# A one-core decoder layer: a v tile's transfer ahead of its slot's others, latent fetches in pairs, and a half swap behind q's parts

## The chip, the cores and the metric

The kernel runs on one core of one Trainium2 chip. A core has a matrix engine (TensorE, PE in the profile, with PEld for its weight loads), VectorE (DVE), ScalarE (ACT), GpSimd (POOL), and SyncE (SP), which here does nothing but issue transfers. The engines run their own instruction streams in order and wait for each other through semaphores; transfers are carried out by 16 DMA engines. The metric is the time of one execution on the device in microseconds, as the median of several runs.

## The reference

One layer of a decoder over 512 tokens of width 2048, in float32. What matters here:

```python
h = rmsnorm(x, attn_norm_g) * (1.0 + scale) + shift          # scale, shift, gate from silu(c) @ w_ada + b_ada
q_lat, kv_lat, k_rope, z_mla, u, v, z_sgu, g_mla, g_sgu = split_cols(h @ w_in, IN_SPLITS)
q  = rmsnorm(q_lat, q_norm_g) @ w_uq        # 16 heads of 128 plain + 64 rotary columns
kv = rmsnorm(kv_lat, kv_norm_g) @ w_ukv     # 16 heads of 128 (k) + 128 (v)
y_mla = causal_attention(q, k, v) * silu(z_mla)
vn = rmsnorm(v, sgu_norm_g)                 # 16 groups of 128 columns, 4 chunks of 128 tokens
mixed = einsum('gts,bnsgd->bntgd', tril(w_spatial), vn) + b_spatial
y_sgu = u * mixed * silu(z_sgu)
x = x + gate * ((sigmoid(g_mla) * y_mla + sigmoid(g_sgu) * y_sgu) @ w_out)
return rmsnorm(x, final_norm_g)
```

The rotary part swaps the halves of each head's 64 columns: `[t1*cos - t2*sin, t2*cos + t1*sin]`.

## The kernel before

Every product is made in float32 precision out of three matmuls on a high and a low part of each operand. For each weight tile ACT casts the high part (`L629` in the mixing loop, `L118` in the streamed stages) and DVE subtracts it to make the low part (`L136`, `L119`); PE then runs high x high, low x high, high x low. So PE needs, for each weight tile, first ACT and then DVE to be done.

The work goes in stages:

- The first two products over all of `x`: the latents of q and k/v, and the columns that a block of the next stage would not hold. They leave for DRAM.
- **The mixing loop** (`L1352` to `L1388`): 11 blocks of weight columns (v, u, the gates) in a seven-product scheme of the Strassen kind, with 28 steps each. A step is 12 matmuls of 128x512 on one weight tile (`L1384` to `L1386`). The weights come through buffers `X0`, `X1`, `X5` (blocks that pass), `X4` and `wraw0` to `wraw2` (blocks that are kept and added to). Their parts go to `w0`, `w1` and one more pair of `X` buffers in rotation.
- Between the steps lie side jobs: the 16 groups of the gating unit, bias sums, rotary tables, and the normalisation of the latents. A side job is put at a step and a phase with `on(step, phase, f)`. In each step `run` goes through FIRST, HIGH, EVAC, GATE, SPLIT, BACK before the step's matmuls are recorded, and through MISC and LOAD after them. What is recorded first stands first in its engine's queue. `place` looks for a step with room on DVE, by a table of costs. Nothing else orders the work: the engines run what they were given in that order.
- **Attention** over 16 heads, with weights through a stream of three raw buffers (`Stream`), then the output product and the last norm.

A group g of the gating unit has these parts: `gain_load` and `v_load` fetch a gain row and a 128x512 tile of v from DRAM (`v_d`), four steps later `sgu_scale` (ACT, `L928`) multiplies v by its norm, DVE multiplies the group's spatial weights by a triangle (`sgu_weights`, `wsr`) which ACT and DVE split, DVE multiplies by the gain, and `sgu_split` makes `sinT` and `vl`, v's high and low parts. `sgu_mix` is one product of three matmuls on PE, in phase MISC. All groups use one buffer for v, `lat12`: the next `v_load` has to wait until DVE has made `vl` of the group before. It is put at the step of that group's mix, in phase LOAD, in which weight transfers of the mixing loop are issued as well.

The normalised latents (ten tiles of 128x512, `latn_d`) are fetched back by `lat_fetch` from step `s_att` on, which is step -11 counted from the loop's end, and split by `lat_split` (ACT `L1313`, DVE `L139`) in the last seven steps; 8 and 9 follow behind the loop. The last weight block of the loop is issued at step -9. At the loop's end SP also issues the rotary tables, the shared rotary key (`kr_d`) and the first weights of attention.

The first head pair begins with `rproj(0)` (rotary queries), `qproj(0)`, `kproj(0)` and `vproj(0)`. `qproj` takes its weights, calls `meanwhile`, records its 18 matmuls, calls `then`, and records q's high and low parts:

```python
    def swapped(m2, src):
        for b in range(4):
            s_, d_ = slice(32 * b, 32 * b + 32), slice(32 * (b ^ 1), 32 * (b ^ 1) + 32)
            ACT.copy(m2[d_], src[s_])
```

SP's transfers also share eight completion semaphores in rotation, so that a transfer waits for the landing of the one eight before it.

Of the kernel before, what the change touches and what calls it, by code (L numbers as in the profile page):

```python
# [128 lines left out]
def trunk_layer(ctx, tc, xT, xn, c, vecs, pos, wada, w1, w2, wv, wv3, wv4, wh, wh15, wq, wqr, wk, wvv, wo, wsT, bsp, gfin, out,  # L129
# [17 lines left out]
    def mm3(ps, ah, al, bh, bl, start, stop):  # L147
        PE.matmul(ps, ah, bh, start=start, stop=False)  # L148
        PE.matmul(ps, ah, bl, start=False, stop=False)  # L149
        PE.matmul(ps, al, bh, start=False, stop=stop)  # L150

    def hilo(hi, lo, src):
        ACT.copy(hi, src)
        tt(lo, src, hi.bitcast(F32), ALU.subtract)
# [28 lines left out]
    ws = Stream(nc, [(wp, f"wraw{i}") for i in range(3)], [(wp, f"w{i}") for i in range(2)])  # L183
# [83 lines left out]
    gq, gr, gk, gvv = {}, {}, {}, {}  # L267
# [45 lines left out]
    def get(i, ahead=1, run=1):  # L313
        r = ws.get(i, ahead)
        fs, pend[:] = pend[:run], pend[run:]
        for f in fs:
            f()
        return r
# [11 lines left out]
    def bank():  # L330
        n_bank[0] += 1
        return bank_at(ring[(n_bank[0] - 1) % len(ring)])
# [368 lines left out]
    FIRST, HIGH, EVAC, GATE, SPLIT, BACK, MISC, LOAD = range(8)  # L701

    def on(s, phase, f, *a):
        assert s >= done[0], (s, done)
        events.setdefault(s, {}).setdefault(phase, []).append(lambda: f(*a))
# [7 lines left out]
    def place(s, us, f, *a):  # L713

        def full(s):
            own, (a, b) = busy.get(s, 0.0) + us, (busy.get(s + d, 0.0) for d in (-1, 1))
            near = [sum(busy.get(s + d + k, 0.0) for k in range(5)) for d in range(-4, 1)]
            return own > 3.3 or own + max(a, b) > 5.75 or s < at_block[T0] + 22 and max(near) + us > 13.4

        while full(s):  # L720
            s += 1
        spend(s, us)
        on(s, BACK, f, *a)
        return s
# [141 lines left out]
    last_gates = []  # L866
    for b in range(1, len(BLOCKS)):
# [21 lines left out]
        if ta == "z":  # L889
            for half in range(2):  # L890
                s_ = max(ready[ta, ca, half], ready[tb_, cb, half]) + 1
# [68 lines left out]
    for c in range(4):  # L960
        for half in range(2):
            s_ = ready["u", c, half]
            for ty in sorted("st", key=lambda t: ready[t, c, half]):
                s_ = place(max(s_, ready[ty, c, half]) + 1, 1.22, t_gate, c, ty, half)
                gated[ty, c, half] = s_
            gated[c, half] = s_
    s_ = at_block[T0] + 6
    on(s_, LOAD, sgu_load, 0)
    out_at = {-2: s_, -1: s_}
    for g in range(H):  # L970
        c, q = divmod(g, 4)
        on(s_, LOAD, gain_load, g)
        on(s_, LOAD, v_load, g)
        a = s_ + 4
        on(a, BACK, sgu_scale)
        a = place(a, 0.29, sgu_weights)
        a = place(a, 0.29, sgu_weights_split)
        if g + 1 < H:
            on(a + 1, LOAD, sgu_load, g + 1)
        a = place(max(a, s_ + 5), 0.69, sgu_gain)  # L980
        a = place(a + 1, 0.69, sgu_split)
        s_ = max(a + 1, out_at[g - 2], max(ready["u", c, half] for half in range(2)) - 2)
        on(s_, MISC, sgu_mix, g)
        for half in range(2):
            out_at[g] = place(max(s_ + 1, ready["u", c, half] + 1), 0.46, sgu_out, g, half)
            last_out[g, half] = out_at[g]
        if q == 3:
            for half in range(2):
                stored[c, half] = max(last_out[k, half] for k in range(4 * c, g + 1)) + 1
                stored[c, half] = max(stored[c, half], gated[c, half] + 1)  # L990
                on(stored[c, half], LOAD, t_store, c, half)
# [143 lines left out]
    def to_bias(s, q):  # L1135

        on(s, MISC, shift_turn, 4 * q)
        return place(s + 1, 0.6, shift_sum, 4 * q)

    used, biased = [rope_end + 3] * 3, []  # L1140
    s_ = used[0]
    for i, (q, ks, _) in enumerate(shares):
        on(used[-3], LOAD, share_load, i)
        s_ = place(max(used[-3] + 4, s_ + 1), 0.75 if len(ks) == 1 else 1.4, share, i)
        used.append(s_)
        if ks[-1] == KC - 1:
            s_ = to_bias(s_ + 1, q)
# [66 lines left out]
    s_ = s_rx + 4  # L1214
    for group in (((10, "lat8"), (11, "lat9")), ((12, "lat10"), ("plain", "sinT"))):
        for i, t in group:
            on(free_at[t], LOAD, lat_load, i, t, z_d if i == "plain" else None)
        for i, _ in group:
            if i == "plain":
                s_ = place(s_ + 1, 0.69, plain_gate)  # L1220
            else:
                s_ = place(max(s_, s_bias) + 1, 0.69, lat_scale, i)
                on(s_ + 1, BACK, last_sigmoid, i)
                s_ = place(s_ + 2, 0.69, last_gate, i)
        i = group[0][0]
# [3 lines left out]
    for lo_, hi_, dim in ((0, 6, 768), (6, 10, 512)):  # L1229
# [6 lines left out]
        for i in range(lo_, hi_):  # L1236
            s_ = place(max(loaded[i] + 4, s_ + 1), 0.69, lat_scale, i)
# [3 lines left out]
        s_ = added  # L1241
        on(s_ + 1, MISC, lat_sums, dim)
        s_ = place(s_ + 2, 1.3, lat_recip)
        s_ += 1
        on(s_, MISC, lat_rstd)
        for i in range(lo_, hi_):
            s_ = place(s_ + 1, 0.75, lat_norm, i)
# [33 lines left out]
# [5 lines that stand above are left out]
# [7 lines left out]
    s_ = s_lat + 1  # L1293
    on(s_, LOAD, key_load)
    s_ += 5
    for i in range(3):
        s_ = place(s_ + 1, 0.69, key_rotary, i)
# [35 lines left out]
    s_att = max(V7.index((2, 3)) + 1 - n_v, s_lat + 1)  # L1333
    on(s_att, LOAD, to_attention)
    for i in range(10):
        on(s_att + i // 3, LOAD, lat_fetch, i)
        if i < 8:
            on((-7, -7, -5, -5, -3, -3, -2, -2)[i], BACK, lat_split, i)

# [67 lines left out]
    def at(name, dt, shape=(P, S)):  # L1407
        p, tag = place[name]
        if p is latp.p:
            v = slot(tag, dt)  # L1410
            return v if len(shape) == 2 else v.rearrange("p (n w) -> p n w", n=shape[1])
        return nt(p, list(shape), dt, tag)
# [67 lines left out]
    def qproj(h, meanwhile=None, then=None):  # L1480
        wH, wL = get(gq[h])
        if meanwhile:
            meanwhile()
        ps = bank()
        for k in range(6):
            sl = slice(k * P, (k + 1) * P)
            mm3(ps, wH[:, sl], wL[:, sl], lh[k], ll[k], k == 0, k == 5)
        if then:
            then()
        qh, ql = at("qh", F32R), at("ql", F32R)  # L1490
        hilo(qh, ql, ps)
        qt[h] = (qh, ql)

    def rproj(p):
        wH, wL = get(gr[p])
        ps = bank_at(0)
        for k in range(6):
            sl = slice(k * P, (k + 1) * P)
            mm3(ps, wH[:, sl], wL[:, sl], lh[k], ll[k], k == 0, k == 5)
        return ps  # L1500
# [12 lines left out]
    def kproj(h):  # L1513
        wH, wL = get(gk[h])
        ps = bank()
        for k in range(4):
            sl = slice(k * P, (k + 1) * P)
            mm3(ps, wH[:, sl], wL[:, sl], lh[6 + k], ll[6 + k], k == 0, k == 3)
        return ps
# [127 lines left out]
    fetch(0)  # L1647
    rps = rproj(0)
    m2 = at("m2", F32)
    qproj(0, lambda: (swapped(m2, rps), [f() for f in last_gates]), lambda: ws.split_to(gvv[0]))  # L1650
    ps = kproj(0)
    kfinish(0, ps)
    rfinish(0, rps, m2)
# [12 lines left out]
    for h in range(H):  # L1666
# [8 lines left out]
        if more:  # L1675
            qproj(h + 1, lambda: merge(1 if h == H - 2 else None))
            if not odd and 2 * pair < H:
                rps = rproj(pair)
# [33 lines left out]
        if not odd and 2 * pair < H:  # L1712
            m2 = at("m2", F32)
# [69 lines left out]
    def residual(n, part, sl, ps, last=False):  # L1783
        y = yt[:, n, sl]
        w = sl.stop - sl.start
        t = nt(tp, [P, S], F32, "sig", bufs=3)[:, :w]
        tt(t, ps, grow[:, sl], ALU.mult)
        tt(y, t, y, ALU.add)
        junk = nt(tp, [P, S], F32, "sig", bufs=3)[:, :w]
        ACT.activation(junk, y, AF.Square, accum_out=ssy[:, n, part:part + 1])  # L1790
        if not last:
            tt(y, y, gfb[:, sl], ALU.mult)

    for cg in range(3):
# [6 lines left out]
        for n in range(NB):  # L1801
            f = lambda n=n, cg=cg, ps=pso[n]: residual(n, cg, slice(cg * 512, (cg + 1) * 512), ps)
# [107 lines left out]
```

## Time and profile before

| | |
|---|---|
| median of 3 runs | 1571.46 us (1569.64 to 1572.58) |
| profiled execution, its own time | 1570.91 us |
| its span, first to last instruction | 1569.2 us |
| mean granted TensorE clock | 0.998 |
| moved from and to HBM | 291.11 MB read, 23.68 MB written |

In the profile's rows the first number is the start in microseconds from the span's start, the second the duration, then engine, line of the kernel, operation, `out<-in`, shape and count. In square brackets stands how long the engine was idle before the row and what ended that. Rows of SPq are transfers being issued: their duration is that of the issue, not of the transfer. The chain of work that ended last follows PE through most of the span.

### The profile page before, as it was taken

What the parts mean: (1) busy time and instruction counts of PE and PEld (TensorE: products, weight loads), DVE (VectorE), ACT (ScalarE), POOL (GpSimd) and SP (SyncE); (2) the same over time, 40 slices, a digit from 0 to 9 for tenths busy, and PEclk for the clock granted to TensorE, in tenths of its full rate; (3) what the DMA queues carried; (4) which work ended last, traced back from release to release, by engine and by line L of the source; (5) the groups of instructions that cost most, each with busy time, mean ns of one, the idle gap of its engine ahead of it and who ended that gap; (6) DMA issues with size and microseconds to landing.
All of it is one profiled execution on the core that took longest, in us unless ns stands there. A gap on an engine that the chain in (4) does not pass through costs nothing.

```text
span 1569.2 us, 20577 instructions
## 1 busy us (share of the span) xinstructions
PE 1554.3 (99%) x7392; PEld 1297.0 (83%) x7392; DVE 1218.4 (78%) x1667; ACT 803.1 (51%) x1238; POOL 69.8 (4%) x67
## 2 busy tenths in 40 slices
PE   9999999999999999999999999999999999999998
PEld 8888778888888888888788888887888888888887
DVE  8989777678887879788879797878777777865763
ACT  4445555546545555445455565657655565532332
POOL 0000000201010101020100010100000000000000
PEclk9999999999999999999999999999999999999999
DMA  9989565949795968686867685966443433348722
GB/s 378 374 278 346 162 192 159 246 131 260 214 241 162 244 203 227 196 230 188 226 178 204 204 251 161 260 166 207 152 118 116 130 118 118 93 133 332 264 89 107
DMA packets 237224, 316.16 MB, mean 201 GB/s; under 512 B 16201, under 2 KB 184193, under 8 KB 231489
## 3 DMA queue, kind: packets, MB, share of 16 engines
q1 hardware_dynamic: 214210, 291.78, 56.7%
q0 software_dynamic: 22912, 23.07, 9.5%
q8 instruction: 58, 0.95, 0.3%
q14 instruction: 44, 0.36, 0.1%
HBM read 291.11 MB, written 23.68 MB: 201 GB/s over the span
## 4 chain that ended last, share of the span: by engine, by line
PE 60%; DVE 2%; DMA 2%; ACT 1%; issue 1%; SPq 0%; DVEq 0%; ACTq 0%
PE ps L1386 10%; PE ps L1384 10%; PE ps L1385 10%; PE ps L149 9%; PE ps L150 9%; PE ps L148 9%; PE ps L1600 1%; PE ps L1626 1%; DMA X<-in_wh 1%; PE ps L1560 1%; PE ps L1561 1%; DMA lat<-v_d 0%; DVE d L136 0%; DMA rx<-kr_d 0%; DVE w1l L136 0%
## 5 line engine op out<-in xcount | busy, mean ns | idle before, releaser
L136 DVE TENSOR_TENSOR X<-X,X 128x1024 fp32r<-128x1024 f32 (+2 forms) x111 | 130.5, 1182 | 31.1 <-ACT X L629 29.5
L629 ACT CAST X<-X 128x1024 fp32r<-128x1024 f32 x70 | 73.7, 1052 | 98.1 <-PE ps L1385 60.9
L629 ACT CAST w0h<-X 128x1024 fp32r<-128x1024 f32 x70 | 73.7, 1052 | 98.0 <-PE ps L1385 49.2
L629 ACT CAST w1h<-X 128x1024 fp32r<-128x1024 f32 x69 | 72.6, 1052 | 75.1 <-PE ps L1385 40.8
L136 DVE TENSOR_TENSOR w0l<-X,w0h 128x1024 fp32r<-128x1024 f32 x70 | 85.5, 1222 | 29.4 <-ACT w0h L629 29.2
L136 DVE TENSOR_TENSOR w1l<-X,w1h 128x1024 fp32r<-128x1024 f32 x69 | 84.3, 1221 | 24.7 <-ACT w1h L629 24.6
L136 DVE TENSOR_TENSOR X<-wraw,X 128x1024 f32<-128x1024 f32 (+1 forms) x65 | 79.4, 1221 | 20.8 <-ACT X L629 18.4
L119 DVE TENSOR_TENSOR w0l<-wraw,w0h 128x1024 fp32r<-128x1024 f32 (+4 forms) x61 | 64.2, 1053 | 40.3 <-ACT w0h L118 38.3
L118 ACT CAST w1h<-wraw 128x1024 fp32r<-128x1024 f32 (+4 forms) x60 | 50.5, 841 | 84.2 <-PE ps L150 21.9
L1386 PE MATMUL ps<-w1l,hh 128*128 128x512 f32 x236 | 92.0, 390 | 1.5 <-DVE w1l L136 1.4
L118 ACT CAST w0h<-wraw 128x1024 fp32r<-128x1024 f32 (+4 forms) x61 | 56.0, 918 | 72.4 <-PE ps L150 21.1
L1386 PE MATMUL ps<-X,hh 128*128 128x512 f32 x232 | 90.6, 391 | 1.5 <-DVE X L136 1.5
L1384 PE MATMUL ps<-w1h,hh 128*128 128x512 f32 x236 | 92.0, 390 | 0.0
L1385 PE MATMUL ps<-w1h,hl 128*128 128x512 f32 x236 | 91.9, 389 | 0.0
L1385 PE MATMUL ps<-w0h,hl 128*128 128x512 f32 x236 | 91.8, 389 | 0.0
L1384 PE MATMUL ps<-w0h,hh 128*128 128x512 f32 x236 | 91.8, 389 | 0.0
L1386 PE MATMUL ps<-w0l,hh 128*128 128x512 f32 x236 | 91.8, 389 | 0.0
L1384 PE MATMUL ps<-X,hh 128*128 128x512 f32 x232 | 90.4, 390 | 0.0
L1385 PE MATMUL ps<-X,hl 128*128 128x512 f32 x232 | 90.3, 389 | 0.0
L139 DVE SCALAR_TENSOR_TENSOR wada<-wada,cact 128x2048 f32<-128x2048 f32 x39 | 88.9, 2282 | 0.6 <-DMA wada<-in_wada 0.6
L119 DVE TENSOR_TENSOR w1l<-wraw,w1h 128x1024 fp32r<-128x1024 f32 (+4 forms) x60 | 57.4, 957 | 34.3 <-ACT w1h L118 33.4
L148 PE MATMUL ps<-hh,w1h 128*128 128x512 f32 x204 | 81.3, 399 | 0.0
(410 smaller groups left out, 4419.7 us busy)
## 6 DMA issues: line engine op xcount, KB each, us to landing
X<-in_wh SPq DMA_DIRECT2D x131, 512.0 KB, 5.0
wada<-in_wada SPq DMA_DIRECT2D x39, 1024.0 KB, 7.6
wraw<-in_wo SPq DMA_DIRECT2D x32, 512.0 KB, 4.1
wraw<-in_wh SPq DMA_DIRECT2D x21, 512.0 KB, 5.5
wraw<-in_wh POOLq DMA_DIRECT2D x21, 512.0 KB, 7.2
X<-in_wv SPq DMA_DIRECT2D x17, 512.0 KB, 3.7
X<-in_wh SPq DMA_DIRECT2D x22, 384.0 KB, 5.2
wraw<-in_w SPq DMA_DIRECT2D x16, 512.0 KB, 9.7
```

What stands on the lines that cost most here:

```text
L118: self.nc.scalar.copy(hi[:, :n], raw[:, :n])
L119: self.nc.vector.tensor_tensor(out=lo[:, :n], in0=raw[:, :n], in1=hi[:, :n].bitcast(F32), op=ALU.subtract)
L136: DVE.tensor_tensor(out=out, in0=in0, in1=in1, op=op)
L139: DVE.scalar_tensor_tensor(out=out, in0=in0, scalar=scalar, in1=in1, op0=op0, op1=op1, **kw)
L148: PE.matmul(ps, ah, bh, start=start, stop=False)
L149: PE.matmul(ps, ah, bl, start=False, stop=False)
L150: PE.matmul(ps, al, bh, start=False, stop=stop)
L629: ACT.copy(hi, t)
L1384: PE.matmul(ps[t].rearrange("p (h w) -> p h w", h=4), xh[:, tk], wH[:, k], start=st, stop=False, skip_group_check=True)
L1385: PE.matmul(ps[t].rearrange("p (h w) -> p h w", h=4), xl[:, tk], wH[:, k], start=False, stop=False, skip_group_check=True)
L1386: PE.matmul(ps[t].rearrange("p (h w) -> p h w", h=4), xh[:, tk], wL[:, k], start=False, stop=sp, skip_group_check=True)
L1560: PE.matmul(ps, q2[:, q], krh[:, :n], start=False, stop=False)
```

## The change

Three places are edited.

```diff
     for g in range(H):
         c, q = divmod(g, 4)
+        on(s_, MISC, v_load, g)
         on(s_, LOAD, gain_load, g)
-        on(s_, LOAD, v_load, g)
...
     for i in range(10):
-        on(s_att + i // 3, LOAD, lat_fetch, i)
+        on(s_att + (0, 0, 2, 2, 4, 4, 5, 5, 6, 6)[i], LOAD, lat_fetch, i)
...
-    qproj(0, lambda: (swapped(m2, rps), [f() for f in last_gates]), lambda: ws.split_to(gvv[0]))
+    qproj(0, lambda: [f() for f in last_gates], lambda: ws.split_to(gvv[0]))
+    swapped(m2, rps)
```

First, `v_load` goes from phase LOAD to phase MISC of the same step, so that it is issued ahead of every other transfer of that step. In SP's queue it changes places with the gain row in every group, with weight transfers in nine (1, 3, 4, 7, 8, 9, 11, 12 and 15), with the spatial weights in group 0, and with a store of `t_d` in groups 5 and 13. In SP's queue group 12 (the transfer from `v_d`) stood behind two weight tiles in four transfers and the gain row:

```order
L1012 DMA half0_932_6268<-in_wh 128x512
L594 DMA wraw1_936_6291<-in_wh 128x3x256
L599 DMA wraw1_936_6291<-in_wh15 128x2x128
L594 DMA X5_937_6294<-in_wh 128x3x256
L599 DMA X5_937_6294<-in_wh15 128x2x128
L910 DMA gsr_938_6297<-gain_row_107 128x128
L914 DMA lat12_939_6299<-v_d_111 128x4x128
L594 DMA X0_942_6319<-in_wh 128x3x256
```

and stands now right behind the transfer of the bias sums (`half0`):

```order
L1012 DMA half0_932_6268<-in_wh 128x512
L914 DMA lat12_936_6291<-v_d_111 128x4x128
L594 DMA wraw1_937_6293<-in_wh 128x3x256
L599 DMA wraw1_937_6293<-in_wh15 128x2x128
L594 DMA X5_938_6296<-in_wh 128x3x256
L599 DMA X5_938_6296<-in_wh15 128x2x128
L910 DMA gsr_939_6299<-gain_row_107 128x128
L594 DMA X0_942_6319<-in_wh 128x3x256
```

The v transfer has moved ahead by five transfers; the order of the others is unchanged.

Second, the ten latents are fetched two at a time over seven steps instead of three at a time over four. In SP's queue (`b6` to `b15` are the latents' tiles, `X1` the mixing loop's last weight block, `wraw0` takes the rope-query weights, `wraw1` q's) stood before

```order
L1306 DMA b6_1318_8613<-latn_d0_127 128x512
L1306 DMA b7_1319_8615<-latn_d1_128 128x512
L1306 DMA b8_1320_8617<-latn_d2_129 128x512
L1306 DMA b9_1323_8637<-latn_d3_130 128x512
L1306 DMA b10_1324_8639<-latn_d4_131 128x512
L1306 DMA b11_1325_8641<-latn_d5_132 128x512
L594 DMA X1_1328_8661<-in_wh 128x4x256
L1306 DMA b12_1329_8663<-latn_d6_133 128x512
L1306 DMA b13_1330_8665<-latn_d7_134 128x512
L1306 DMA b14_1331_8667<-latn_d8_135 128x512
L1306 DMA b15_1336_8689<-latn_d9_136 128x512
L99 DMA wraw0_48_8717<-in_wqr 128x768
```

and now

```order
L1306 DMA b6_1318_8613<-latn_d0_127 128x512
L1306 DMA b7_1319_8615<-latn_d1_128 128x512
L594 DMA X1_1324_8653<-in_wh 128x4x256
L1306 DMA b8_1325_8655<-latn_d2_129 128x512
L1306 DMA b9_1326_8657<-latn_d3_130 128x512
L1306 DMA b10_1337_8705<-latn_d4_131 128x512
L1306 DMA b11_1338_8707<-latn_d5_132 128x512
L99 DMA wraw0_48_8709<-in_wqr 128x768
L1306 DMA b12_1341_8727<-latn_d6_133 128x512
L1306 DMA b13_1342_8729<-latn_d7_134 128x512
L1306 DMA b14_1349_8761<-latn_d8_135 128x512
L1306 DMA b15_1350_8763<-latn_d9_136 128x512
```

The weight block stands behind two latents instead of six, and the rope-query weights ahead of the last four.

Third, the half swap of the first rotary queries (four copies of 32x512 on ACT) is recorded behind `qproj(0)` instead of inside it. In ACT's queue (`w1h_50` is a part of k's weights, `w0h_51` of the value weights, `d1` and `d2` the high parts of q and k) stood before

```order
L118 CAST w1h_50_8909<-wraw2_50_8809 128x512
L1285 COPY hl11_1373_8908<-ps0_1372_8889 32x512 x4
L118 CAST w0h_51_8942<-wraw0_51_8854 128x1024
L153 CAST d1_1375_8946<-ps3_1374_8923 128x512
L153 CAST d2_1384_8978<-ps4_1383_8965 128x512
```

and now

```order
L118 CAST w1h_50_8909<-wraw2_50_8809 128x512
L118 CAST w0h_51_8938<-wraw0_51_8854 128x1024
L153 CAST d1_1375_8942<-ps3_1374_8919 128x512
L1285 COPY hl11_1373_8908<-ps0_1372_8889 32x512 x4
L153 CAST d2_1384_8978<-ps4_1383_8965 128x512
```

The four swap copies have moved behind two casts. PE's and DVE's own orders, and POOL's, are unchanged in all three places.

## The prediction

> **What bounds the kernel now.** I read the page first, for the engine that has no room left, then who PE waited for, then the timelines of PE, ACT, DVE and SP around each wait.
>
> ```profile
> span 1569.2 us, 20577 instructions
> ...
> PE 1554.3 (99%) x7392; PEld 1297.0 (83%) x7392; DVE 1218.4 (78%) x1667; ACT 803.1 (51%) x1238; POOL 69.8 (4%) x67
> ```
>
> PE is busy 99% of the span, and no edit touches a matmul. So only the places where PE stands can be won, some microseconds out of 1569. The view of PE's waits puts all of them behind weight parts that DVE made late; its longest single row is
>
> ```profile
> PE ps L1386 <- DVE w1l L136: 1.4, 1, 1.4
> ```
>
> PE's timeline tells what each place really costs, since after a wait the pipeline also restarts.
>
> ```profile
> 538.58 0.39 PE L1384 MATMUL ps<-X,hh 128*128 128x512 f32 x1
> ...
> 543.09 0.40 PE L1384 MATMUL ps<-w1h,s 128*128 128x512 f32 x1
> ...
> 769.77 0.39 PE L1384 MATMUL ps<-w1h,hh 128*128 128x512 f32 x1
> ...
> 781.94 0.40 PE L1384 MATMUL ps<-w1h,s 128*128 128x512 f32 x1
> ...
> 1066.23 0.39 PE L1384 MATMUL ps<-w1h,hh 128*128 128x512 f32 x1
> ...
> 1074.39 0.47 PE L1384 MATMUL ps<-w1h,hh 128*128 128x512 f32 x1
> ...
> 1078.93 0.39 PE L1384 MATMUL ps<-w0h,hh 128*128 128x512 f32 x1
> ...
> 1093.08 0.28 PE L148 MATMUL ps<-w0h,hh 128*128 128x256 f32 x1
> 1093.78 0.39 PE L149 MATMUL ps<-w0l,hh 128*128 128x256 f32 x1 [0.42 <-DVE w0l L119]
> ```
>
> Undisturbed, three steps of 12 matmuls run from 1066.23 to 1074.39: 8.16 us, so 2.72 a step and 0.227 a matmul. From 538.58 to 543.09 stand one step and a mix (15 matmuls, 3.41 us) in 4.51: 1.1 us lost. From 769.77 to 781.94 stand three steps and a mix (39 matmuls, 8.85) in 12.17: 3.3 lost. From 1074.39 to 1078.93 one step in 4.54: 1.8 lost. At 1093.08 another 0.42 of idle. These 6.6 us are what the three edits can reach.
>
> **Edit 1, the v tile's transfer first.** One SP instruction moves per group, 16 in all; none is added. It passes the weight transfers, the gain row and in two groups a store of `t_d`.
>
> ```profile
> 519.52 0.37 SPq L594 DMA_DIRECT2D wraw<-in_wh  x1
> ...
> 521.03 0.43 SPq L914 DMA_DIRECT2D lat<-v_d  x1
> ...
> 752.89 0.54 SPq L1012 DMA_DIRECT2D half<-in_wh  x1
> 757.62 0.37 SPq L594 DMA_DIRECT2D wraw<-in_wh  x1
> ...
> 760.52 0.43 SPq L914 DMA_DIRECT2D lat<-v_d  x1
> ```
>
> ```profile
> 527.52 1.28 ACT L928 ACTIVATE lat<-lat,rv 128x128 f32<-128x128 f32 x4 [1.47 <-DMA lat<-v_d]
> ...
> 766.37 1.28 ACT L928 ACTIVATE lat<-lat,rv 128x128 f32<-128x128 f32 x4 [3.68 <-DMA lat<-v_d]
> ...
> 769.77 1.28 ACT L857 ACT_TABLE_LOAD   x1
> 771.07 1.06 ACT L857 ACTIVATE d<-d 128x1024 f32<-128x1024 f32 x1
> 772.03 1.03 ACT L629 CAST w0h<-wraw 128x1024 fp32r<-128x1024 f32 x1
> ```
>
> ```profile
> 527.45 0.28 DVE L136 TENSOR_TENSOR wsr<-wsr,tri 128x128 f32<-128x128 f32 x1
> ...
> 750.47 0.69 DVE L136 TENSOR_TENSOR vl<-lat,sinT 128x512 fp32r<-128x512 f32 x1
> ...
> 764.70 0.28 DVE L136 TENSOR_TENSOR wsr<-wsr,tri 128x128 f32<-128x128 f32 x1
> ...
> 773.10 1.23 DVE L136 TENSOR_TENSOR w0l<-wraw,w0h 128x1024 fp32r<-128x1024 f32 x1 [2.66 <-ACT w0h L629]
> ...
> 780.63 0.68 DVE L136 TENSOR_TENSOR vl<-lat,sinT 128x512 fp32r<-128x512 f32 x1
> ```
>
> Group 12 first. SP is idle from 753.4 until a weight buffer comes free at 757.62; the v transfer stands behind that and leaves at 760.52, lands 5.8 us later, and ACT's scaling of v, at the head of ACT's queue, waits 3.68 us for it. All weight casts stand behind it. Now the v transfer comes right behind `half`, and its tile is free once DVE has split group 11 (750.47 + 0.69 = 751.16): it leaves at 753.5 and with the same 5.8 lands at 759.3, before ACT gets there (766.37 - 3.68 = 762.69). The scaling then ends at 763.97. The next cast, of the mix weights, waits for the product with the triangle (764.70 + 0.28 = 764.98) and starts at 765.0 instead of 766.37 + 1.28 = 767.65. So ACT's queue moves 2.6 us, the w0h cast from 772.03 to 769.4, and DVE's w0l from 773.10 to 770.5. From there to the end of vl (781.31) DVE runs eight operations back to back, so that end moves by 2.6 too, and PE, which waits for vl at the mix, gets 2.6 of its 3.3 us.
>
> This holds only if ACT's function switch costs what its row shows: 1.28 us, and the next instruction starts at 771.07, 0.02 behind it. The Trainium skill (ScalarE: Activation LUTs, What ACT_TABLE_LOAD costs) gives about 1.28 us for the load and 1.38 for a drain with each switch. By that rule w0h would come 1.4 later, this term would be 1.2 and the whole sum 4.5; the rows show the load and no such drain, so I keep 2.6.
>
> Group 4 has the same form. Its v transfer leaves by 519.52, where the displaced weight transfer stood, so 1.5 before 521.03, which covers the 1.47 of ACT's idle time. The next cast again waits for a product, until 527.73 instead of 528.80: the queue moves 1.07, against 1.1 lost by PE there. I take 1.0 (between 0, if DVE has its own backlog, and 1.1).
>
> Against it: where v's tile is still being read, SP now stands at the v transfer with weights behind it. The widest case is
>
> ```profile
> 611.48 0.37 SPq L594 DMA_DIRECT2D X<-in_wh  x1
> ...
> 613.62 0.37 SPq L914 DMA_DIRECT2D lat<-v_d  x1
> ```
>
> The v transfer left at 613.62, as soon as it could. The weight block that it now precedes leaves at 614.1, 2.6 later than 611.48. I cost it at nothing, since PE lost no time behind it and a block is loaded several steps of 2.72 us ahead; two steps of cover gone would cost up to 2.6. The gain row, passed in all groups, is needed after the scaling and costs nothing. POOL's own queue keeps its order.
>
> **Edit 2, the latents two at a time.** Ten fetches of 256 KB stay ten. Four of the six that stood ahead of the last weight block move behind it, and four move behind the rope-query weights.
>
> ```profile
> 1058.75 2.96 SPq L1306 DMA_DIRECT2D b<-latn_d  x6
> 1061.83 0.51 SPq L594 DMA_DIRECT2D X<-in_wh  x1
> ...
> 1067.09 0.33 SPq L99 DMA_DIRECT2D wraw<-in_wqr  x1
> ```
>
> ```profile
> 1056.26 1.22 DVE L136 TENSOR_TENSOR X<-X,X 128x1024 f32<-128x1024 f32 x1
> ...
> 1075.25 1.22 DVE L136 TENSOR_TENSOR w1l<-wraw,w1h 128x1024 fp32r<-128x1024 f32 x1
> ...
> 1089.65 2.35 DVE L136 TENSOR_TENSOR d<-d,d 128x1024 f32<-128x1024 f32 x2
> ```
>
> ```profile
> 1068.42 1.05 ACT L629 CAST X<-X 128x1024 fp32r<-128x1024 f32 x1 [2.62 <-DMA X<-in_wh]
> ...
> 1076.39 2.56 ACT L1313 ACTIVATE hh<-b,vec 128x512 fp32r<-128x512 f32 x4
> ...
> 1089.04 2.35 ACT L1285 COPY hl<-ps 32x512 f32<-32x512 f32 x4
> 1091.41 1.05 ACT L118 CAST w0h<-wraw 128x1024 fp32r<-128x1024 f32 x1
> ```
>
> The block's buffer is free when the sum at 1056.26 ends (1057.48), yet the block leaves at 1061.83, behind six issues of 0.49 us. Behind two it leaves at 1058.75 + 0.98 = 1059.75. Even with the same 6.5 us to landing (1068.3 - 1061.83) it lands at 1066.25, just when PE stops reading the buffer of the cast (1066.23, the next step's first matmul). So the cast moves from 1068.42 to about 1066.3, 2.1 earlier, and with it the chain on ACT and DVE to w1l, whose end goes from 1076.47 to 1074.4. PE wants it with the third matmul of its step, at 1074.39 + 0.45 = 1074.84: the 1.8 us are gone, with 0.4 to spare. The wait that comes next, PE's for the first rope-query low part, shrinks as well, but I count nothing for it: the value weights below bind that stretch again.
>
> The last four fetches now leave behind 1067.09, from 1067.5 to 1069, and land by about 1075 (6 us, an estimate from the block's 6.5). Latents 6 and 7 are cast second among the four at 1076.39, from 1077.8 then, 1075.7 in the new frame. Cost zero, with about 1 us to spare.
>
> **Edit 3, the half swaps later.** Four ACT copies (2.35 us) move from ahead of the value weights' cast to behind q's own cast. The value cast then starts when PE has finished q (12 matmuls of 0.227 before 1093.08: 1090.36), not at 1091.41, and ends at 1091.4. Its low part then waits for DVE's gate products, which end at 1092.00, and starts there instead of at 1092.46: 0.5 of gain, against 0.42 idle and the restart at 1093.78. The casts of k and the rotation of q come 1 to 2 us later; they lie under the value projection, 48 matmuls of half width from 1093.08 on, about 6 us.
>
> **Sum.** 2.6 + 1.0 + 1.8 + 0.5 = 5.9 us. The profiled execution took 1570.91, which gives 1565.0; the median of the runs, 1571.46, is 0.55 above it, which gives 1565.6. I forecast 1565.6.
>
> **The rivals.** A difference under 0.2% (3.1 us) can't be told from no change.
> - The latents bring nothing: their bytes are the same, and if the 6.5 us are bandwidth, the block may land as late as before. Then 1571.46 - 4.1 = 1567.4. Against it, four fetches fewer stand ahead of the block.
> - The v tile brings nothing: in two groups a weight that had to wait behind it is wanted at once, and what ACT wins is lost again. Then 1571.46 - 2.3 = 1569.2. Where the largest gain is, at 753.4, the tile was free 2 us before.
> - New waits for DVE, which is busy 78%, take everything back: about 1571.
> - The latents turn into a wait: 6 to 9 now stand behind the rope-query weights, whose buffer DVE frees. For the weights after those SP stood 9.0 us:
>
> ```profile
> SPq L99 <- DVE w1l L136: 9.0, 1, 9.0
> ```
>
>   If the release at 1067.09 slips by more than the 1 us to spare, each further one holds the start of attention; a slip of 9.0 would end at 1571.46 - 5.9 + 8.0 = 1573.6, not to be told from before. Against it, nothing ahead of that release on DVE gets later.
> - Slower: SP standing at the v tile, 2.6 us in group 8, is the rule, and the weights behind have no cover. Each such group then costs up to 2.6; from the third on it decides (5.9 / 2.6 = 2.3), and four of the 16 end at 1571.46 - 5.9 + 10.4 = 1576.0. For it, any tile of a group whose predecessor is split just then; against it, PE showed no wait near 611.
>
> **Chances.** The forecast 0.55, with 1564.0 to 1566.8 as its own range; the latents bring nothing 0.16; the v tile brings nothing 0.10; all taken back 0.05; the latents wait 0.05; slower 0.09. Faster by over 0.2% (below 1568.3) are the first two: 0.71; the next three are the same: 0.20; slower 0.09. The range goes from all 6.6 us and the restarts won (1563.6) up to 1570.4, between the third case and the fourth.
>
> **What the profile after would show.** Edit 1: ACT's scaling of groups 4 and 12 without idle time before it, and no PE wait between 765 and 782; wrong if the scaling still waits, or a weight cast waits for a transfer behind 611. Edit 2: the block leaves about 2 us after the first fetch's 1058.75 less the shift, ACT's X cast waits for PE instead of a DMA, and the 1.4 wait is gone; wrong if 6 or 7 is waited for. Edit 3: the value weights' cast ahead of the swaps, and PE's wait at that place under 0.2. The forecast fails if a new row of PE's waits of over 1 us appears.

## The result, and the profile after

The changed kernel takes 1565.32 us (median, 1565.21 to 1567.51) against 1571.89 us (1569.64 to 1573.48) of the kernel before, measured beside it. The ratio is 0.9962, with a 95% interval of 0.9949 to 0.9975: 6.0 us are won by the ratio, between 3.9 and 8.0; the two medians differ by 6.6. The forecast was 1565.6. The profiled execution took 1566.76 us, 1.4 above the median, so it is not the best witness of the sum, but it shows each place.

The page and the view of PE's waits of the kernel after:

```profile
span 1565.1 us, 20574 instructions
...
PE 1552.7 (99%) x7392; PEld 1296.2 (83%) x7392; DVE 1218.7 (78%) x1667; ACT 802.9 (51%) x1238; POOL 70.5 (5%) x67
```

```profile
PE ps L443 <- ACT hh L430: 1.7, 2, 0.9
...
PE ps L1386 <- DVE X L136: 0.2, 1, 0.2
PE ps L1386 <- DVE w1l L136: 0.2, 1, 0.2
```

The waits of the mixing loop for weight parts, 1.4 us the longest of them before, are down to 0.2. What stays largest in sum is a wait of the first product, which no edit touches: 0.7 before, 1.7 now, 1.8 with the v tile alone and 2.1 with the latents alone, though that product is the same in all of them. It is not the new row by which the forecast would have failed, and it costs next to nothing: PE comes out of that product at most 0.2 us later than in the trace of before.

PE's timeline of the kernel after, at the places that the prediction reads (group 4's step and mix, group 12's, the loop's end, the value projection):

```profile
539.70 0.39 PE L1384 MATMUL ps<-X,hh 128*128 128x512 f32 x1
...
543.31 0.40 PE L1384 MATMUL ps<-w1h,s 128*128 128x512 f32 x1
...
770.01 0.39 PE L1384 MATMUL ps<-w1h,hh 128*128 128x512 f32 x1
...
779.45 0.40 PE L1384 MATMUL ps<-w1h,s 128*128 128x512 f32 x1
...
1063.72 0.39 PE L1384 MATMUL ps<-w1h,hh 128*128 128x512 f32 x1
...
1071.88 0.39 PE L1384 MATMUL ps<-w1h,hh 128*128 128x512 f32 x1
...
1075.10 0.39 PE L1384 MATMUL ps<-w0h,hh 128*128 128x512 f32 x1
...
1089.23 0.28 PE L148 MATMUL ps<-w0h,hh 128*128 128x256 f32 x1
1089.36 0.39 PE L149 MATMUL ps<-w0l,hh 128*128 128x256 f32 x1
```

The same stretches now take less, and the difference is the gain at each place. "Alone" is the same difference in the profiles of kernels with one edit, shown below.

| place | before | after | gained | forecast | alone |
|---|---|---|---|---|---|
| group 4, one step and the mix | 4.51 | 3.61 | 0.90 | 1.0 | 0.91 |
| group 12, three steps and the mix | 12.17 | 9.44 | 2.73 | 2.6 | 2.76 |
| loop's end, one step | 4.54 | 3.22 | 1.32 | 1.8 | 1.82 |
| first to second product of the value weights | 0.70 | 0.13 | 0.57 | 0.5 | 0.59 |

That is 5.5 us; 0.2 of them are given back 7 us later, where PE's steps from the value projection to the first scores take 0.22 longer than before. The two profiled executions differ by only 1570.91 - 1566.76 = 4.15, since the one after lost about 1 us ahead of all this: PE reaches the step that starts at 393.93 before only at

```profile
394.90 0.50 PE L1384 MATMUL ps<-w0h,s 128*128 128x512 f32 x1 [0.40 <-ACT d L842]
```

Some 0.6 us of it are lost here, the rest earlier. The v tile of group 0 is fetched at this place, so this could have been a price of the first edit. It isn't. ACT's copy of `d`, for which PE waits, stands behind a cast that waits 3.35 us, until 393.32, for a weight transfer; SP had issued that one at 381.37, ahead of the first v tile (392.84), and up to that tile SP's order is as before. The runs below say the same.

### The profile page after: what moved, and what is told of

Its sections match the earlier page's. It is cut to its first block, busy times and chain, and to the rows that moved or that the text cites. A ratio compares the mean times of both kernels' runs of the same rounds, so it can differ in the third digit from the quotient of the medians.

```text
span 1565.1 us, 20574 instructions
## 1 busy us (share of the span) xinstructions
PE 1552.7 (99%) x7392; PEld 1296.2 (83%) x7392; DVE 1218.7 (78%) x1667; ACT 802.9 (51%) x1238; POOL 70.5 (5%) x67
## 4 chain that ended last, share of the span: by engine, by line
PE 91%; DMA 3%; DVE 3%; ACT 1%; issue 1%; SPq 0%; DVEq 0%; ACTq 0%
PE ps L1384 16%; PE ps L1386 16%; PE ps L1385 16%; PE ps L149 12%; PE ps L150 12%; PE ps L148 12%; PE ps L443 5%; DMA X<-in_wh 2%; PE ps L1600 1%; PE ps L1626 1%; DMA wraw<-in_w 1%; PE ps L1560 1%; PE ps L1561 1%; DVE X L136 1%; DVE d L136 0%
```

## The experiments

### Each edit alone

The v tile first:

```diff
+        on(s_, MISC, v_load, g)
         on(s_, LOAD, gain_load, g)
-        on(s_, LOAD, v_load, g)
```

> Only the v tile's transfer goes first in its step; latents and half swap as before. If each part acts at its own place: 3.6 us faster than before, about 1567.9; ACT's scaling of v in groups 4 and 12 without idle time, and PE ahead by about 0.8 us behind group 4's mix and 2.5 us more behind group 12's. If SP's standing at the v tile costs something in the other groups: PE falls behind by 0.5 us or more at one of them, and the whole is under 3 us. If the parts share their gain (the three waits hide each other): more than 3.6, since later waits then shrink as well.

Measured: 1567.47 us, ratio 0.9975 (0.9966 to 0.9984), so 3.9 us won. PE's timeline of this kernel, group 4 and group 12:

```profile
538.97 0.39 PE L1384 MATMUL ps<-X,hh 128*128 128x512 f32 x1
...
542.57 0.39 PE L1384 MATMUL ps<-w1h,s 128*128 128x512 f32 x1
...
769.22 0.39 PE L1384 MATMUL ps<-w1h,hh 128*128 128x512 f32 x1
...
778.63 0.39 PE L1384 MATMUL ps<-w1h,s 128*128 128x512 f32 x1
```

3.60 and 9.41 us: the two gains, 0.91 and 2.76, with 1.4 us of PE's wait at the loop's end left as it was. Nothing was lost at group 0 here, though the edit is the same. In the trace the parts act each at its own place.

The latents two at a time:

```diff
-        on(s_att + i // 3, LOAD, lat_fetch, i)
+        on(s_att + (0, 0, 2, 2, 4, 4, 5, 5, 6, 6)[i], LOAD, lat_fetch, i)
```

> Only the latents are fetched two at a time. If each part acts at its own place: the stall of PE at the third last step of the mixing loop shrinks from 1.6 us by 1.4 to 1.8, about 1569.9, and nothing else moves. If the weight block's flight is set by bandwidth: it leaves 1.7 us earlier and lands as late as before, and the stall stays, 1571.5. If the last latents wait behind the rope-query weights: ACT's casts of latents 6 and 7 show idle time that a transfer ends, and the time is 1571.5 or above.

Measured: 1569.51 us, ratio 0.9987 (0.9978 to 0.9996), 2.0 us won. SP's timeline of this kernel, the view of the block's transfer (its last number is the time from issue to landing), ACT's and PE's timelines, and PE's view of waits:

```profile
1058.60 1.01 SPq L1306 DMA_DIRECT2D b<-latn_d  x2
1059.71 0.38 SPq L594 DMA_DIRECT2D X<-in_wh  x1
```

```profile
X<-in_wh SPq DMA_DIRECT2D x1, 512.0 KB, 6.0
```

```profile
1066.52 1.05 ACT L629 CAST X<-X 128x1024 fp32r<-128x1024 f32 x1 [0.96 <-PE ps L1385]
```

```profile
1066.50 0.39 PE L1384 MATMUL ps<-w1h,hh 128*128 128x512 f32 x1
...
1074.66 0.39 PE L1384 MATMUL ps<-w1h,hh 128*128 128x512 f32 x1
...
1077.38 0.39 PE L1384 MATMUL ps<-w0h,hh 128*128 128x512 f32 x1
```

```profile
PE ps L149 <- DVE w0l L119: 0.7, 1, 0.7
```

The block leaves 1.11 us behind the first latent, its cast waits for PE and for nothing else, and the step takes its undisturbed 2.72 us: all 1.82 are won. ACT's latents 6 and 7 wait for no transfer. The wait at the value weights grows from 0.4 to 0.7, as the forecast had it ("the value weights below bind that stretch again").

The half swap behind q's parts:

```diff
-    qproj(0, lambda: (swapped(m2, rps), [f() for f in last_gates]), lambda: ws.split_to(gvv[0]))
+    qproj(0, lambda: [f() for f in last_gates], lambda: ws.split_to(gvv[0]))
+    swapped(m2, rps)
```

> Only the half swap goes behind q's parts. If each part acts at its own place: 0.5 us, about 1571.0, too little for the times, to be read from PE's idle time at the first low product of the value projection (0.42 us before, under 0.2 then) and from how far PE is ahead behind it. If the rotation of q or the casts of k, which come later, are wanted at once: PE waits anew within the next 10 us and the 0.5 us are gone.

Measured: 1571.21 us, ratio 1.000 (0.9992 to 1.0009). The times can't tell it. PE's timeline:

```profile
1093.49 0.28 PE L148 MATMUL ps<-w0h,hh 128*128 128x256 f32 x1
1093.60 0.38 PE L149 MATMUL ps<-w0l,hh 128*128 128x256 f32 x1
```

The 0.42 us of idle time are gone and 0.59 won, of which 0.2 are lost again 7 us later, in this kernel as in the full change. About 0.4 stay in the trace, which no time here can confirm.

The three ratios alone come to 3.9 + 2.0 + 0.0 = 5.9 us, the whole change to 6.0. Each of the three is uncertain by about 1.4 us, so the times show no more than that the parts roughly add up.

### Where the v tile's gain comes from, and what standing costs

Only groups 4 and 12, and then all others:

```diff
+        if g in (4, 12):
+            on(s_, MISC, v_load, g)
         on(s_, LOAD, gain_load, g)
-        on(s_, LOAD, v_load, g)
+        if not (g in (4, 12)):
+            on(s_, LOAD, v_load, g)
```

> The v tile's transfer goes first in groups 4 and 12 alone; in the other fourteen groups, the latents and the swap all is as before. If the gain comes from these two groups and the other fourteen cost nothing: the same 3.6 us as with all groups moved, about 1567.9. If the other fourteen groups cost PE time (0.7 us appeared at group 0 in the profile after): 0.7 us or more faster than with all groups moved, 1567.2 or below.

Measured: 1568.24 us, ratio 0.9976 (0.9966 to 0.9985), as with all groups moved (0.9975). In PE's timeline the two stretches take 3.59 and 9.46 us, as with all groups moved. The two groups are the whole gain, as far as times and trace can tell.

The other kernel has the condition turned round (`g not in (4, 12)`).

> The v tile's transfer goes first in the fourteen groups other than 4 and 12, with all else as before. If SP's standing at the v tile costs nothing: the time of the kernel before, 1571.2 within 1.0, and PE keeps step with the trace of before to 0.3 us at each of the fourteen mixes, though weight blocks leave up to 2.6 us later. If standing has a price: PE falls behind at groups 3, 8 or 11 by up to 2.6 us each, 1573 or above.

Measured: 1571.43 us, ratio 1.0001 (0.9992 to 1.001). SP's timeline at group 8 shows it standing as foretold:

```profile
614.12 0.37 SPq L914 DMA_DIRECT2D lat<-v_d  x1
614.53 0.50 SPq L594 DMA_DIRECT2D X<-in_wh  x1
```

The weight block leaves at 614.53 instead of 611.48. PE itself is 0.5 us behind the trace of before here, so measured against PE the block leaves 2.6 us later, as reckoned. PE's lag is 0.0 us from group 0 to group 4 and 0.5 from there to group 12, and PE is 0.25 ahead from there on: it changes at the two groups that this kernel leaves as they were, and at none of the fourteen. What is lost at 394.90 in the profile of the full change is not there either, nor in the two other profiles with the same edit at group 0 (the v tile alone, and the next one).

A longer stand, the transfer a whole step earlier:

```diff
-        on(s_, LOAD, v_load, g)
+        on(s_ - (g > 0), MISC, v_load, g)
```

> The v tile's transfer goes first of the step ahead of the one it has in the change (all groups but the first), so SP stands at it for a whole step, 2.7 us, longer wherever the tile is not yet free: this doubles the suspected cost. If the weights behind have cover: as with the change's first edit alone, 1567.5, with up to 0.5 more. If the cover is thin: each group in which SP stands costs up to 2.6 us of PE time; from the second on the gain of 3.6 is gone, and eight such groups give 1580 and above.

Measured: 1567.50 us, ratio 0.9976 (0.9967 to 0.9986), the same as with the edit alone. Group 13's weights, in SP's timeline of the kernel before, and its v tile with the weights behind it in that of this kernel:

```profile
778.36 0.37 SPq L594 DMA_DIRECT2D X<-in_wh  x1
```

```profile
777.40 0.37 SPq L914 DMA_DIRECT2D lat<-v_d  x1
777.82 0.65 SPq L594 DMA_DIRECT2D X<-in_wh  x1
```

PE is 3.9 us ahead of before at that place, so measured against PE the weights leave 3.4 us later, more than a whole step of 2.72 us, and PE doesn't wait for them. Behind the v tiles of groups 5, 6, 9 and 14 weights leave up to 3.4, 1.9, 2.8 and 2.4 us later than before, measured in the same way, and PE loses nothing there either. In group 8 it is 2.6 us as with the edit alone, for SP issues nothing in the step between: there the cost was not doubled. In the groups where SP stood longer the weights had cover for it; the slower rival's mechanism is there, but its price in these runs is nothing.

### What sets the last block's landing

Four latents ahead of the block instead of two:

```diff
-        on(s_att + i // 3, LOAD, lat_fetch, i)
+        on(s_att + (0, 0, 1, 1, 4, 4, 5, 5, 6, 6)[i], LOAD, lat_fetch, i)
```

> Four latents ahead of the last weight block (six before, two with the change), the v tile and the half swap as before. If the issues ahead of the block set its landing: it leaves 1.0 us after the time with two, lands 1.0 later, its cast comes about 0.8 later than with two, and PE regains 0.8 to 1.0 of the 1.7 us, about 1570.3. If bandwidth sets it: its landing doesn't follow its issue and the gain is none, 1571.2, or that with two, 1569.5.

Measured: 1570.39 us, ratio 0.9991 (0.9982 to 1.0001). The time hits the first expectation, but it is no help at this size, and the traces show that the expectation missed. SP's, ACT's and PE's timelines:

```profile
1059.73 0.38 SPq L594 DMA_DIRECT2D X<-in_wh  x1
```

```profile
1065.62 1.05 ACT L629 CAST X<-X 128x1024 fp32r<-128x1024 f32 x1 [1.17 <-PE ps L1386]
```

```profile
1073.62 0.39 PE L1384 MATMUL ps<-w1h,hh 128*128 128x512 f32 x1
...
1076.34 0.39 PE L1384 MATMUL ps<-w0h,hh 128*128 128x512 f32 x1
```

The step takes 2.72 us: four ahead win as much as two, all 1.8 us and not 0.8 to 1.0. PE is 1.0 us ahead of the trace with two here (1073.62 against 1074.66), so against PE the block left 1.1 us later, although the two issues stand at almost the same time. It landed within 5.9 us (by 1065.62), and its cast still waited for PE alone. The gain ends where the cast is bound by PE, and four is enough for that.

None ahead:

```diff
+        on(s_att + (2, 2, 2, 2, 4, 4, 5, 5, 6, 6)[i], LOAD, lat_fetch, i)
```

> No latent ahead of the last weight block, the v tile and the half swap as before. If the block's cast is bound by PE once two latents stand ahead of it: the block leaves 1 us earlier, its cast stays within 0.2 us of that with two, and the gain is the same 1.7 us, 1569.5. If the first latents, which now leave later, hold back ACT's queue (they stand ahead of the block's cast in it): ACT waits 0.5 us or more for them and PE gets 0.5 us less, 1570.0 or above.

Measured: 1570.34 us, ratio 0.9989 (0.998 to 0.9999). ACT's and PE's timelines:

```profile
1066.75 1.41 ACT L1313 ACTIVATE hh<-b,vec 128x512 fp32r<-128x512 f32 x2 [2.51 <-DMA b<-latn_d]
...
1069.01 1.04 ACT L629 CAST X<-X 128x1024 fp32r<-128x1024 f32 x1
```

```profile
1077.10 0.50 PE L1386 MATMUL ps<-w1l,hh 128*128 128x512 f32 x1 [0.96 <-DVE w1l L136]
```

Now the first latents are late. They stand ahead of the block's cast in ACT's queue, which waits 2.51 us for them, and the cast follows without idle time once they are through: it is ACT's queue that binds it now, not the block. PE's wait is back at 0.96, and the step takes 3.97 us, so only 0.6 of the 1.8 us are won. The second theory holds, and its price is larger than the 0.5 us I had put on it.

Two ahead, the other eight right behind the block:

```diff
+        on(s_att + (0, 0, 2, 2, 2, 2, 2, 2, 3, 3)[i], LOAD, lat_fetch, i)
```

> Two latents ahead of the last weight block as in the change, the other eight right behind it instead of in pairs over later steps; v tile and half swap as before. If the number of fetches ahead of the block sets its landing: it leaves where it does with the change's fetches, its cast waits for PE alone, and the whole 1.7 us are won, 1569.5. If the bytes in flight beside it set its landing (the fetches behind it too): its flight grows from 6.0 us to 7 or more, the cast waits for the transfer and at most 0.9 us are won, 1570.4 or above.

Measured: 1570.02 us, ratio 0.9987 (0.9977 to 0.9996). The view of the block's transfer, and PE's timeline:

```profile
X<-in_wh SPq DMA_DIRECT2D x1, 512.0 KB, 7.0
```

```profile
1075.59 0.39 PE L1384 MATMUL ps<-w1h,hh 128*128 128x512 f32 x1
...
1078.35 0.39 PE L1384 MATMUL ps<-w0h,hh 128*128 128x512 f32 x1
```

A split verdict. The flight is 7.0 us, as the theory of the bytes beside it said, and the cast waits for the transfer; yet the step takes 2.76, so 1.78 us are won. The longer flight is absorbed by what the block had to spare. Whether the followers lengthened it is not shown, since the full change, with the same two ahead and fewer close behind, has 6.8.

Six ahead, the last four out of the way:

```diff
+        on(s_att + (0, 0, 0, 1, 1, 1, 5, 5, 6, 6)[i], LOAD, lat_fetch, i)
```

> Six latents ahead of the last weight block as before, and only the last four moved behind the rope-query weights; v tile and half swap as before. If the number of fetches ahead sets the landing: the block leaves 3.1 us behind the first fetch and takes 6.5 us as before, and nothing is won, 1571.3. If the bytes in flight beside it set it: the flight shrinks by 0.7 us or more, since no latents follow, and PE regains as much, 1570.6 or below.

Measured: 1571.41 us, ratio 0.9994 (0.9985 to 1.0003). The view of the block's transfer:

```profile
X<-in_wh SPq DMA_DIRECT2D x1, 512.0 KB, 6.4
```

The flight stays at 6.4 us (6.5 before) with no latent behind the block: taking the followers away doesn't speed it up by more than flights differ between profiles. PE's stall here is 1.35 us against 1.82 in the profile of before. That is no proof of a gain, for the profile of the half swap alone, whose fetches are as before, has 0.98 there. What moves the landing is when the block leaves: behind six fetches 3.9 to 5.1 us ahead of PE's step (the one at 1066.23 before) in the seven profiles that have them, behind two 6.1 to 6.8 in four, while the flights overlap (5.9 to 6.7 and 6.0 to 7.0 us). The Trainium skill (DMA: Bandwidth & Descriptors, Queues, rings and completion order) says that SP's transfers use one ring on each of the DMA engines and that descriptors are consumed in ring order. By that rule alone followers would cost the block nothing, and 6.4 against 6.5 agrees, while the 7.0 us with eight followers don't fit it as well, if they are more than scatter.

### The rival of the waiting latents, made to happen

```diff
+        on(s_att + (0, 0, 2, 2, 4, 4, 7, 7, 8, 8)[i], LOAD, lat_fetch, i)
```

> The change's fetches, but the last four one transfer later still, behind q's weights, which left at about 1074.6 with the change's fetches; v tile and half swap as before. This makes the rival in which the latents wait. If their 1 us to spare is real and all there is: latents 6 and 7 land at about 1079, ACT stands 2 to 4 us at their casts with the rope-query casts behind, and PE loses 2 to 3.5 us: 1571.5 to 1573. If more lies ahead of their use than I read: 1569.5 as with the change's fetches.

Measured: 1571.14 us, ratio 0.9995 (0.9985 to 1.0004). ACT's and PE's timelines:

```profile
1078.15 0.73 ACT L1313 ACTIVATE hh<-b,vec 128x512 fp32r<-128x512 f32 x1 [2.60 <-DMA b<-latn_d]
1079.80 0.72 ACT L1313 ACTIVATE hh<-b,vec 128x512 fp32r<-128x512 f32 x1 [0.92 <-DMA b<-latn_d]
...
1081.29 0.50 PE L148 MATMUL ps<-hh,w1h 128*128 128x512 f32 x1 [1.32 <-ACT w1h L118]
```

ACT stands 3.5 us and PE waits 1.32 for the rope-query weights that it casts next. Most of the gain of the fetches is taken back. One transfer further back is enough for that, because it means 7.5 us: the last four leave from 1074.70 on, against 1067.21 with the change's fetches. PE's wait is shorter than the 2 us or more expected, and the time stays under 1571.5.

## Why the prediction was right, point by point

**Group 12.** The chain came as written. SP's and ACT's and DVE's timelines of the kernel after:

```profile
753.77 0.38 SPq L914 DMA_DIRECT2D lat<-v_d  x1
```

```profile
762.83 1.28 ACT L928 ACTIVATE lat<-lat,rv 128x128 f32<-128x128 f32 x4
765.04 0.30 ACT L153 CAST whl<-wsr 128x128 fp32r<-128x128 f32 x1 [0.94 <-DVE wsr L136]
...
767.27 1.28 ACT L857 ACT_TABLE_LOAD   x1
768.57 1.06 ACT L857 ACTIVATE d<-d 128x1024 f32<-128x1024 f32 x1
769.54 1.03 ACT L629 CAST w0h<-wraw 128x1024 fp32r<-128x1024 f32 x1
...
770.60 1.23 DVE L136 TENSOR_TENSOR w0l<-wraw,w0h 128x1024 fp32r<-128x1024 f32 x1 [2.67 <-ACT w0h L629]
```

The next cast was forecast at 765.0 and stands at 765.04, w0h at 769.4 and 769.54, w0l at 770.5 and 770.60. That these times agree so closely is luck: about 1.1 us lost ahead of group 4 and 0.9 won there leave PE 0.24 us behind the trace of before (770.01 against 769.77). The lengths of the stretch, 12.17 and 9.44, are free of that. PE still waits 0.2 us for vl, where the prediction expected no wait. The function switch again shows its 1.28 us and the next instruction 0.02 behind it. The 1.2 us that this term would have been by the rule of the drain don't fit the 2.73 here and 2.76 alone.

**Group 4.** 1.0 forecast, 0.90 and 0.91 measured; ACT's scaling has no idle time before it:

```profile
527.08 1.27 ACT L928 ACTIVATE lat<-lat,rv 128x128 f32<-128x128 f32 x4
```

The v transfer left at 516.45, ahead of 519.52 by more than I had counted, which changes nothing, since ACT's next cast waits for a product.

**Standing at the v tile, costed at nothing.** Right, and with a margin: where SP stood up to a step longer still, that cost nothing that can be seen. Behind group 8's stand, from 611 to 632, no weight cast of ACT waits for a transfer.

**The latents.** 1.8 forecast, 1.82 alone, but 1.32 in the profile of the full change. The step that failed there is "even with the same 6.5 us to landing (1068.3 - 1061.83) it lands at 1066.25, just when PE stops reading the buffer". SP's and ACT's timelines of the kernel after, and the transfer's own time:

```profile
1056.54 1.01 SPq L1306 DMA_DIRECT2D b<-latn_d  x2
1057.66 0.38 SPq L594 DMA_DIRECT2D X<-in_wh  x1
```

```profile
X<-in_wh SPq DMA_DIRECT2D x1, 512.0 KB, 6.8
```

```profile
1064.55 1.05 ACT L629 CAST X<-X 128x1024 fp32r<-128x1024 f32 x1 [0.20 <-DMA X<-in_wh]
```

The block left 1.1 us behind the first latent, as forecast; but the flight took 6.8, and the first latent itself stood 0.3 nearer to PE's step. So the cast came 0.83 us behind PE's step (1063.72) instead of with it. PE lost 0.50 of that; before, 1.82 of 2.19; with the half swap alone, 0.98 of 1.35 (cast 1068.81, PE's step 1067.46). In all three the loss is the lateness less 0.33 to 0.37: that is the 0.4 to spare of the forecast. It also explains why eight followers, with a cast 0.3 us late, lose nothing. So the mechanism held and the size is 1.3 to 1.8, by how the transfer falls.

**The latents behind the rope-query weights, costed at nothing.** Right: no wait for 6 and 7. But the 1 us to spare was too small an estimate. With the latents alone, latent 8, issued behind both at 1068.16, took 4.9 us instead of the 6 assumed and landed at 1073.1, while the cast of latent 6 begins at about 1075.8. That leaves some 2.7 us, if 6 and 7 landed no later than 8. The run above shows where it ends: moved by 7.5 us, the two hold ACT for 3.5.

**The swap.** 0.5 forecast, 0.57 and 0.59 measured. What the forecast left out are the 0.2 given back at the first scores; "under the value projection, 48 matmuls of half width" did not cover quite everything.

Two readings of the prediction were off without harm. The view of PE's waits doesn't put all of them behind weight parts: 1.1 us for POOL's `mask`, 0.7 for ACT's `hh` and 0.6 for DVE's `hl` are in it too, and no edit was to win these. And the lower end of the range, 1563.6, is not what the working gives: 1571.46 less all 6.6 us, which hold the restarts but for the last place's, is 1564.9.

The sum of 5.9 stands against 5.5 less 0.2 in the profiles and 6.0 in the times. Its small errors lean both ways, and the agreement of the median to 0.3 us is better than the measurement can vouch for.

## What to carry to other kernels

When the bounding engine is at 99%, look for its few stalls, and follow each back to the transfer that leaves too late: often not the transfer's length but what stands ahead of it in an in-order queue is what can be changed. A gain of this kind ends where the next releaser binds, so ask how far that is: two and four fetches ahead did equally well, and none ahead moved the wait to the consumer's own queue. An early wait in the issuing queue is cheap as long as what stands behind it has more cover than the wait lasts, and a trial with the wait made longer shows that better than an argument, once the trace confirms where it did get longer.

## What the runs showed that was not expected

The same 512 KB block, issued behind the same two latents, took 6.0 us with this edit alone and 6.8 in the full change; behind four latents it landed within 5.9. PE's stall at this place also wandered between profiles in which the fetches are those of before, from 0.98 us (half swap alone) to 1.85. So one profile of a stall that hangs on a transfer gives its size to about half a microsecond here.

The same holds for the two groups. In the nine profiles without the first edit at groups 4 and 12, the one of before among them, ACT's scaling waits 1.28 to 2.55 us at group 4 and 2.59 to 4.31 at group 12, and PE's stretches take 4.33 to 5.15 and 11.06 to 12.80 us. In the four with it ACT waits for nothing there, and the stretches take 3.59 to 3.61 and 9.16 to 9.46. So that both gains exist is beyond the scatter, while their sizes in the table rest on one profile before: by the means of the nine and the four, group 4's gain would be 1.2 instead of 0.9 and group 12's 2.6, together 3.85 against the 3.9 in the times of that edit alone.
